# Nine buffers in place of three for the token rows of the input norm

## The chip, the cores and the metric

The kernel runs on one core of a Trainium2 chip. The metric is device time in microseconds (us) of one execution. Before the change three runs took 2201.86, 2203.27 and 2207.52 us, median 2203.27.

A core has five engines that each work through their own list of instructions in order: PE (TensorE, matrix multiplication), DVE (VectorE), ACT (ScalarE), POOL (GpSimd) and SP (SyncE, which here only issues transfers). They wait for each other by semaphores. Transfers between DRAM and the on-chip memory (SBUF) are moved by 16 DMA engines.

## The reference

One layer of a causal decoder over 16 meta tokens and 1024 real tokens of width 1024, all in float32:

```
h = concat(zeros(112), meta_tokens(16), x(1024))
u = rmsnorm(h, norm_mix_w)
z, xbc, dt, q, k, v, g_ssd, g_att = split(u @ w_in)          # 1024 x 8480
y_ssd = gated_rmsnorm(ssd(silu(conv4(xbc)), dt), z) @ w_ssd_branch
y_att = window_attention(q, k, v, rel_bias, sinks) @ w_attn_branch
h = h + (sigmoid(g_ssd+b0)*y_ssd + sigmoid(g_att+b1)*y_att) @ w_out
h = h + (silu(gate) * up) @ w_down      # (up, gate) = conv3(rmsnorm(h) @ w_ffn_in)
out = rmsnorm(h, norm_final_w)[:, 128:]
```

The attention looks at a window of 128 tokens, the meta tokens and a learned sink. The SSD branch (a state space model) goes through blocks of 128 tokens in order.

## The kernel before, in words

Matrices are split into a high and a low part (`split`, L94 to L96: ACT writes the high part, DVE subtracts and writes the low part), and each product is three matmuls: high by high (L168), low by high (L169) and high by low (L170). A projection job takes 128 columns of `w_in`: `prep` (L141) loads them into one of three `wf` buffers (512 KB, L145) and splits them into `wh` and `wl`; `gemm_slice` multiplies them with the normed tokens `r1h`, `r1l` in three slices of tokens, 24 matmuls each.

The head of the kernel is the loop that the change touches (L231 to L243). It goes over nine blocks of tokens: block 0 with the 16 meta tokens, blocks 1 to 8 with 128 rows of x (512 KB each). SP loads a block into `xt` (L234). `norm_T` then squares and sums it on ACT (L181), scales the sum on DVE (L182), takes its power on POOL (L183), multiplies the rows on DVE into `xn` (L184), transposes them in eight pieces on PE (L189, `ntp`), and splits them into `r1h` (ACT, L95) and `r1l` (DVE, L96). `xt` has three buffers, so a load has to wait until the block three before it has been normed. The loads of `norm_mix_w` (`wb`) and of the weights of K and V stand among those of x. The bias table of the attention (`rb`, `oh`, two matmuls `pg` at L223, `gv`) follows block 3, and the small constants (`rw`, `sel`, `d2`, `nsink`) follow the loop.

Behind the loop K and V are projected for all tokens (slices of 272, 384 and 384 tokens; the first needs blocks 0 to 2, the second 3 to 5, the third 6 to 8). K and V go to DRAM (`k_d`, `v_d`, stores of L294) and come back in another layout (`att_k` L498 in two halves of 1 MB, `att_v` L499, `att_vm` L501). Then 66 projection jobs follow, and between their matmuls run the attention (first matmuls `attS`, L574 and L575) and the SSD (per block: `ssdcb` L700, `ssdE` L708, `ssdpx` L717, `ssdyo` L751, `ssdst` L757, `ssdyd` L770, `ssdss` L789). After them come the branch products, the output projection, the gated MLP and the final norm.

The order of instructions is not written out by hand. A scheduler reads the whole program, plays it through with its own costs, and writes each engine's list; what is issued early or late in that play shifts where the background work (`pull`, attention and SSD) is set among the projections. It uses eight semaphores for transfers in turn: a transfer waits until the one issued eight places before it has landed.

```
            xt = p0.tile([P, D], F32, tag="xt", name="xt", bufs=3)
            sp.dma_start(xt[:n], A["meta_tokens"] if b == 0 else A["x"][P * (b - 1):P * b, :])
            if b in (2, 3):
                pend.append(prep(w_in[:, c0:c0 + P]))
            norm_T(xt, n, t0, wb, p0, ps0, "nt")
```

Of the kernel before, what the change touches and what calls it, by code (L numbers as in the profile page):

```python
# [11 lines left out]
F32 = mybir.dt.float32  # L12
# [6 lines left out]
P = 128  # L19
D = 1024  # L20
# [28 lines left out]
def blk(b):  # L49
    return (0, NM) if b == 0 else (NM + P * (b - 1), P)  # L50
# [36 lines left out]
def body(ctx: ExitStack, tc: tile.TileContext, A, out, keep=None):  # L87
# [52 lines left out]
    def prep(src, m=P, eng=None):  # L140
        wf = wp.tile([P, KC, P], F32, tag="wf", name="wf", bufs=3)  # L141
        wh = wp.tile([P, KC, P], F32R, tag="wh", name="wh", bufs=WB)
        wl = wp.tile([P, KC, P], F32R, tag="wl", name="wl", bufs=WB)
        q = abs(m)
        sp.dma_start(wf[:, :, :q], src.rearrange("(k p) c -> p k c", p=P))  # L145
        if m < 0:
            split(wh[:, :, :q], wh[:, :, q:2 * q], wf[:, :, :q])
        else:
            split(wh[:, :, :m], wl[:, :, :m], wf[:, :, :m], eng)
        return wh, wl, m  # L150
# [41 lines left out]
    def norm_T(xt, n, t0, wb, pl, psp, tagp):  # L192
        for ks, ps in norm_ps(xt, n, wb, pl, psp, tagp):
            split(r1h_[:, ks, t0:t0 + n], r1l_[:, ks, t0:t0 + n], ps)

    def rows(pl, psp, tagp, srcs, dst, name):
        n = sum(s.shape[0] for s in srcs)
        t = pl.tile([P, P], F32, tag="rows", name=name)
        o = 0
        for s in srcs:  # L200
            sp.dma_start(t[o:o + s.shape[0], :], s)
            o += s.shape[0]
        ps = psp.tile([P, 512], F32, tag=tagp, name="rowsT")
        pe.transpose(ps[:, :n], t[:n, :], ident[:n, :n])
        dve.tensor_copy(dst, ps[:, :n])
# [8 lines left out]
    def bias_by_distance(p0, ps0):  # L214
        rb = p0.tile([33, 16], F32, name="rb", bufs=1)
        oh = p0.tile([33, L_BAND + L_M1 + L_M31], F32, name="oh", bufs=1)
        dve.memset(rb, 1.0)
        sp.dma_start(rb[0:32, :], A["rel_bias"])
        sp.dma_start(oh, A["c_oh"])
        gv = p0.tile([16, L_BAND + L_M1 + L_M31], F32, name="gv", bufs=1)  # L220
        for o, n in ((0, 384), (384, 160)):
            pg = ps0.tile([P, 512], F32, tag="nt", name="pg")
            pe.matmul(pg[:16, :n], rb, oh[:, o:o + n], start=True, stop=True)  # L223
            dve.tensor_copy(gv[:, o:o + n], pg[:16, :n])
        sp.dma_start(gv_d, gv)
# [3 lines left out]
    with tc.tile_pool(name="p0", bufs=2) as p0, tc.tile_pool(name="ps0", bufs=4, space=PSUM) as ps0:  # L229
        wb = p0.tile([P, D], F32, name="wb", bufs=1)  # L230
        for b in range(9):  # L231
            t0, n = blk(b)
            xt = p0.tile([P, D], F32, tag="xt", name="xt", bufs=3)
            sp.dma_start(xt[:n], A["meta_tokens"] if b == 0 else A["x"][P * (b - 1):P * b, :])  # L234
            if b == 0:
                sp.dma_start(wb, A["norm_mix_w"].partition_broadcast(P))
            if b in (2, 3):
                c0 = C_K if b == 2 else C_V
                pend.append(prep(w_in[:, c0:c0 + P]))
            norm_T(xt, n, t0, wb, p0, ps0, "nt")  # L240
            if b == BD:
                bias_by_distance(p0, ps0)
        sp.dma_start(tri, A["c_tri"])  # L243
        cw = A["ssd_conv_w"].rearrange("t (c p) -> (t c) p", p=P)
        cb = A["ssd_conv_b"].rearrange("(c p) -> c p", p=P)
        rows(p0, ps0, "nt", [cw, cb], cvw, "rw1")
        dve.tensor_scalar(out=cvw, in0=cvw, scalar1=0.5, scalar2=None, op0=ALU.mult)
        rows(p0, ps0, "nt", [A["ssd_norm_w"].rearrange("(c p) -> c p", p=P),
                             A["gate_b"].rearrange("b (c p) -> (b c) p", p=P)], ngw, "rw2")
        dve.tensor_scalar(out=ngw[:, 16:32], in0=ngw[:, 16:32], scalar1=0.5, scalar2=None, op0=ALU.mult)  # L250
        fw = A["ffn_conv_w"].rearrange("t (c p) -> (t c) p", p=P)
        fb = A["ffn_conv_b"].rearrange("(c p) -> c p", p=P)
        rows(p0, ps0, "nt", [fw[0:88]], fcw[:, 0:88], "rw3")
        rows(p0, ps0, "nt", [fw[88:132], fb], fcw[:, 88:176], "rw4")
        sel = p0.tile([2, P], F32, name="sel", bufs=1)
        sp.dma_start(sel, A["c_sel"])
        d2 = p0.tile([2, 16], F32, name="d2", bufs=1)
        sp.dma_start(d2, A["ssd_d"].rearrange("(c e) -> e c", e=2))
        pd = ps0.tile([P, 512], F32, tag="nt", name="pd")
        pe.matmul(pd[:, :16], sel, d2, start=True, stop=True)  # L260
        dve.tensor_copy(dch, pd[:, :16])
        sp.dma_start(nsink, A["attn_sinks"].partition_broadcast(P))
        dve.tensor_scalar(out=nsink, in0=nsink, scalar1=-1.0, scalar2=None, op0=ALU.mult)
# [1059 lines left out]
```

## Time and profile before

| what | value |
|---|---|
| runs | 2201.86, 2203.27, 2207.52 us; median 2203.27 |
| profiled execution | 2204.14 us, of which the span of the trace is 2202.4 |
| PE | busy 2152.5 us, 98% of the span |
| DVE, ACT, POOL | busy 64%, 40%, 16% |
| granted TensorE clock, mean | 0.991 of full speed |
| DMA | 250.18 MB, 114 GB/s over the span |

Times in the rows are us from the start of the span. A line such as "[1.98 <-DMA nsink]" says how long an engine stood idle before an instruction and what it inferred as the last thing waited for. A PE that is busy is not always at its full clock: the column PEclk gives the share of full speed that was granted.

### The profile page before, as it was taken

What the parts mean: (1) busy time and instruction counts of PE and PEld (TensorE: products, weight loads), DVE (VectorE), ACT (ScalarE), POOL (GpSimd) and SP (SyncE); (2) the same over time, 40 slices, a digit from 0 to 9 for tenths busy, and PEclk for the clock granted to TensorE, in tenths of its full rate; (3) what the DMA queues carried; (4) which work ended last, traced back from release to release, by engine and by line L of the source; (5) the groups of instructions that cost most, each with busy time, mean ns of one, the idle gap of its engine ahead of it and who ended that gap; (6) DMA issues with size and microseconds to landing.
All of it is one profiled execution on the core that took longest, in us unless ns stands there. A gap on an engine that the chain in (4) does not pass through costs nothing. (4 is left out here: it accounts for less than half of the span.)

```text
span 2202.4 us, 35895 instructions
## 1 busy us (share of the span) xinstructions
PE 2152.5 (98%) x14090; PEld 2049.8 (93%) x14090; DVE 1405.1 (64%) x2558; ACT 871.5 (40%) x1701; POOL 361.3 (16%) x303
## 2 busy tenths in 40 slices
PE   7999999999999999999999999999999999989998
PEld 6899999999999999999999999878999999968887
DVE  6576665567775486354245644558888888875566
ACT  4455644446653454253322212324334333441112
POOL 1111111003330131022000000004433444200000
PEclk9999999999999999999999999999999999999999
DMA  6521422247663464364455432434222222353223
GB/s 172 135 74 47 122 73 72 81 110 182 148 149 95 115 160 114 97 155 115 162 164 165 144 96 84 135 115 125 87 76 78 78 86 68 106 182 96 86 67 125
DMA packets 300329, 250.18 MB, mean 114 GB/s; under 512 B 31768, under 2 KB 272306, under 8 KB 299391
## 3 DMA queue, kind: packets, MB, share of 16 engines
q1 hardware_dynamic: 300159, 247.88, 39.4%
q8 instruction: 111, 1.82, 0.3%
q14 instruction: 59, 0.48, 0.1%
HBM read 180.26 MB, written 67.57 MB: 113 GB/s over the span
## 5 line engine op out<-in xcount | busy, mean ns | idle before, releaser
L168 PE MATMUL gacc<-r1h,wh 128*128 128x342 f32 (+4 forms) x1776 | 579.9, 328 | 5.9 <-DVE cv L457 4.5
L169 PE MATMUL gacc<-r1l,wh 128*128 128x342 f32 (+4 forms) x1776 | 582.0, 328 | 2.1 <-DVE ss L182 1.7
L170 PE MATMUL gacc<-r1h,wl 128*128 128x342 f32 (+4 forms) x1776 | 579.0, 327 | 0.0
L168 PEld LDWEIGHTS gacc<-r1h,wh 128*128 128x128 f32 x1776 | 337.7, 190 | 10.2 <-issue 4.9
L169 PEld LDWEIGHTS gacc<-r1l,wh 128*128 128x128 f32 x1776 | 337.9, 190 | 5.8 <-DVE ss L182 1.9
L170 PEld LDWEIGHTS gacc<-r1h,wl 128*128 128x128 f32 x1776 | 338.0, 191 | 2.8 <-issue 0.2
L96 DVE TENSOR_TENSOR wl<-wf,wh 128x1024 fp32r<-128x1024 f32 x97 | 123.2, 1270 | 116.4 <-ACT wh L95 113.4
L95 ACT ACTIVATE wh<-wf 128x1024 fp32r<-128x1024 f32 x115 | 121.0, 1052 | 191.8 <-PE gacc L169 148.7
L457 DVE SCALAR_TENSOR_TENSOR cv<-gacc,cvw,cv 128x346 f32<-128x346 f32 (+2 forms) x216 | 123.8, 574 | 44.6 <-ACT cv L453 41.6
L1278 PE MATMUL dacc<-dh,r1l 128*128 128x512 f32 x336 | 132.3, 394 | 0.0
L1279 PE MATMUL dacc<-dl,r1h 128*128 128x512 f32 x336 | 132.2, 393 | 0.0
L1277 PE MATMUL dacc<-dh,r1h 128*128 128x512 f32 x336 | 131.9, 393 | 0.0
L1283 DVE TENSOR_TENSOR hh<-dacc,hh 128x512 f32<-128x512 f32 x128 | 87.4, 689 | 67.9 <-PE dacc L1279 66.9
L168 PE MATMUL gacc<-r2h,wh 128*128 128x342 f32 x384 | 122.7, 320 | 3.1 <-ACT r1h L95 1.5
L169 PE MATMUL gacc<-r2l,wh 128*128 128x342 f32 x384 | 123.1, 321 | 0.0
L170 PE MATMUL gacc<-r2h,wl 128*128 128x342 f32 x384 | 122.8, 320 | 0.0
L95 ACT ACTIVATE q<-q 128x1024 fp32r<-128x1024 f32 x44 | 46.7, 1061 | 143.9 <-PE uacc L1174 93.4
L183 POOL TENSOR_TENSOR ss<-ss,mhalf 128x1 f32<-128x1 f32 (+2 forms) x18 | 11.1, 617 | 480.7 <-DVE ss L182 470.3
L1144 POOL TENSOR_TENSOR q<-wf 128x512 f32<-128x512 f32 x22 | 67.7, 3076 | 121.0 <-DVE q L96 121.0
L770 PE MATMUL ssdyd<-M,ssdxd 128*128 128x128 f32 (+1 forms) x576 | 79.9, 272 | 0.0
L770 PEld LDWEIGHTS ssdyd<-M,ssdxd 128*128 128x128 f32 (+1 forms) x576 | 76.3, 191 | 2.5 <-issue 0.8
L1189 DVE SCALAR_TENSOR_TENSOR ta<-ra,fcw,ta 128x1024 f32<-128x1024 f32 x44 | 78.0, 1772 | 0.0
(436 smaller groups left out, 5283.2 us busy)
## 6 DMA issues: line engine op xcount, KB each, us to landing
wf<-in_w_in SPq DMA_DIRECT2D x66, 512.0 KB
wf<-in_w_ffn_in SPq DMA_DIRECT2D x44, 512.0 KB
gl<-ga_d SPq DMA_DIRECT2D x72, 171.0 KB
a_d<-ta SPq DMA_DIRECT2D x22, 512.0 KB
wf<-a_d SPq DMA_DIRECT2D x22, 512.0 KB
wf<-in_w_ffn_out SPq DMA_DIRECT2D x22, 512.0 KB
xs_d<-xt SPq DMA_DIRECT2D x16, 520.0 KB
z_d<-zt SPq DMA_DIRECT2D x16, 513.0 KB
```

The lines of the kernel that those rows point to most:

```text
L95: act.activation(hi, src, AF.Copy)
L96: (eng or dve).tensor_tensor(out=lo, in0=src, in1=ff(hi), op=ALU.subtract)
L168: pe.matmul(ps[:m, :n], wh[:, k, :m], rh[k][:, t0:t0 + n], start=k == 0, stop=False)
L169: pe.matmul(ps[:m, :n], wh[:, k, :m], rl[k][:, t0:t0 + n], start=False, stop=False)
L170: pe.matmul(ps[:m, :n], wl[:, k, :m], rh[k][:, t0:t0 + n], start=False, stop=k == KC - 1)
L457: dve.scalar_tensor_tensor(out=t[:, z:m], in0=ps[:, off + z - lag:off + m - lag], scalar=w, in1=t[:, z:m], op0=ALU.mult, op1=ALU.add)
L770: pe.matmul(yd[:, j, :n], u.xd[:n, j, 64 * e:64 * e + P], u.M[:n, i * n:(i + 1) * n], start=e == 0, stop=e == 1)
L1189: dve.scalar_tensor_tensor(out=t, in0=row[:, 2 - lag:2 - lag + SEQ], scalar=w, in1=t, op0=ALU.mult, op1=ALU.add)
L1277: pe.matmul(ps, ah[:, tb], wh[:, cs], start=i == 0, stop=False)
L1278: pe.matmul(ps, al[:, tb], wh[:, cs], start=False, stop=False)
L1279: pe.matmul(ps, ah[:, tb], wl[:, cs], start=False, stop=i == len(cur) - 1)
L1283: dve.tensor_tensor(out=hh[:, b, cs], in0=ps, in1=hh[:, b, cs], op=ALU.add)
```

## The change

The tile `xt` gets nine buffers in place of three, 36 KB per partition in place of 12 KB, so no load of x waits for a norm to release a buffer.

```diff
--- before.py
+++ after.py
@@ -230,7 +230,7 @@
         wb = p0.tile([P, D], F32, name="wb", bufs=1)
         for b in range(9):
             t0, n = blk(b)
-            xt = p0.tile([P, D], F32, tag="xt", name="xt", bufs=3)
+            xt = p0.tile([P, D], F32, tag="xt", name="xt", bufs=9)
             sp.dma_start(xt[:n], A["meta_tokens"] if b == 0 else A["x"][P * (b - 1):P * b, :])
             if b == 0:
                 sp.dma_start(wb, A["norm_mix_w"].partition_broadcast(P))
```

The scheduler writes other lists from it. The instructions are the same in number and kind on every engine. Their order differs in the first part of the program, up to about the seventeenth `ssdss` of 36, and from there on it is the same on all five engines. Four places:

On SP at the start of the program, the loads in the order of issue (`-` before, `+` now):

```order
 L234 DMA xt<-in_x 128x1024 x2
-L145 DMA wf<-in_w_in 128x8x128 x2
+L145 DMA wf<-in_w_in 128x8x128
+L234 DMA xt<-in_x 128x1024
+L145 DMA wf<-in_w_in 128x8x128
 L218 DMA rb<-in_rel_bias 32x16
 L219 DMA oh<-c_oh 33x544
+L234 DMA xt<-in_x 128x1024 x5
 L243 DMA tri<-c_tri 128x128
 L201 DMA rw_331<-in_ssd_conv_w 96x128
-L234 DMA xt<-in_x 128x1024
```

The third block of x is now asked for ahead of V's weights (the second `wf`), and the last five blocks ahead of all the small constants. Since a transfer waits for the one eight places before it, `nsink`, eight places behind the last block of x, waits for that block to land.

On DVE in the changed kernel, from the low part of block 3 to the low part of block 4 (`gv` is the bias table, `ss` and `xn` in the middle are block 5's):

```order
L96 TENSOR_TENSOR r1l<-ntp,r1h 128x4x128
L224 COPY gv<-pg 16x384
L263 TENSOR_SCALAR nsink<-nsink 128x16
L182 TENSOR_SCALAR ss<-ss 128x1
L184 SCALAR_TENSOR_TENSOR xn<-xt,ss,wb 128x1024
L224 COPY gv<-pg 16x160
L96 TENSOR_TENSOR r1l<-ntp,r1h 128x4x128 x2
```

The small operation on `nsink`, which needs its transfer, now stands ahead of the norm of block 5. Before it stood at this place ahead of the one of block 3:

```order
L96 TENSOR_TENSOR r1l<-ntp,r1h 128x4x128 x2
L182 TENSOR_SCALAR ss<-ss 128x1
L263 TENSOR_SCALAR nsink<-nsink 128x16
L96 TENSOR_TENSOR r1l<-ntp,r1h 128x4x128
L182 TENSOR_SCALAR ss<-ss 128x1
L184 SCALAR_TENSOR_TENSOR xn<-xt,ss,wb 128x1024 x2
```

On SP around the reloading of K and V, before:

```order
L544 DMA tab<-gv_d 128x2x256
L546 DMA tab<-gv_d 128x2x16
L145 DMA wf<-in_w_in 128x8x128
L294 DMA v_d<-vs 128x512
L294 DMA v_d<-vs 128x128
L498 DMA att_k<-k_d 64x2x2048 x2
L501 DMA att_vm<-v_d 16x64 x2
L508 DMA att_t_399<-gv_d 8x16
```

and now:

```order
L294 DMA v_d<-vs 128x512
L501 DMA att_vm<-v_d 16x64 x2
L294 DMA v_d<-vs 128x128
L542 DMA tab<-gv_d 128x2x16
L498 DMA att_k<-k_d 64x2x2048 x2
L543 DMA tab<-gv_d 128x2x128
L499 DMA att_v<-v_d 128x8x64
L544 DMA tab<-gv_d 128x2x256
L546 DMA tab<-gv_d 128x2x16
L145 DMA wf<-in_w_in 128x8x128
```

The reload of K now stands ahead of the tables and of the weights of a later job, and that of V follows two places behind it. On PE the first `attS` stands behind 246 projection matmuls, before behind 267.

On PE in the SSD of the second of four groups, before (`ssdyd` of one block of 128 tokens, then parts of the next two):

```order
L770 MATMUL ssdyd<-M,ssdxd_5152 128x128 x8
L708 MATMUL ssdE<-ssdR_5155,ssdL_5156 128x512
L717 MATMUL ssdpx<-ident,xs 128x128 x4
L789 MATMUL ssdss<-ones,qs 128x1
L751 MATMUL ssdyo<-bc,ssdh 128x128 x4
L708 MATMUL ssdE<-ssdR_5160,ssdL_5161 128x512
L700 MATMUL ssdcb<-bc 128x128
L703 MATMUL ssdcb<-ident,bc 128x128
L168 MATMUL gacc<-r1h,wh 128x342
L169 MATMUL gacc<-r1l,wh 128x342
```

and now, behind the same `ssdyd`:

```order
L708 MATMUL ssdE<-ssdR_5160,ssdL_5161 128x512
L789 MATMUL ssdss<-ones,qs 128x1
L757 MATMUL ssdst<-xe_7665,bt_7642 128x512
L757 MATMUL ssdst<-xe_7664,bt_7643 128x512
L717 MATMUL ssdpx<-ident,xs 128x128 x4
L708 MATMUL ssdE<-ssdR_5160,ssdL_5161 128x512
L708 MATMUL ssdE<-ssdR_5155,ssdL_5156 128x512
L751 MATMUL ssdyo<-bc,ssdh 128x128 x4
L700 MATMUL ssdcb<-bc 128x128
L703 MATMUL ssdcb<-ident,bc 128x128
L770 MATMUL ssdyd<-M,ssdxd_5151 128x128 x8
L168 MATMUL gacc<-r1h,wh 128x342
```

Before, 24 projection matmuls stood between that `ssdyd` and the next one; now none does, and 264 of them follow in one piece.

## Rows read from the trace of the kernel before

**Rows 1.** Busy time by stretch: us of each engine, (instructions), PEclk, DMA share, GB/s

```profile
0.00:50.00 50.00, 36.43 (x217) 33.10 (x218) 30.18 (x59) 24.21 (x44) 6.68 (x17) 0.97 0.63 171
50.00:100.00 50.00, 44.87 (x277) 44.35 (x276) 22.70 (x65) 21.44 (x55) 4.98 (x3) 0.93 0.62 146
100.00:636.00 536.00, 535.39 (x3568) 515.92 (x3566) 362.54 (x964) 289.33 (x738) 89.88 (x95) 1.00 0.40 103
636.00:650.00 14.00, 13.46 (x98) 12.57 (x97) 12.65 (x24) 10.85 (x26) 5.66 (x6) 1.00 0.54 128
...
718.00:2202.40 1484.40, 1454.37 (x9494) 1376.53 (x9493) 937.62 (x1383) 501.87 (x799) 249.73 (x176) 0.99 0.38 114
```

**Rows 2.** Waits of PE, whole run: us in total, times, longest

```profile
PE ntp L189 <- DVE xn L184: 8.3, 3, 7.7
PE attS L574 <- DMA att_v<-v_d: 5.1, 1, 5.1
PE gacc L168 <- DVE cv L457: 4.5, 2, 4.1
...
PE gacc L169 <- DVE ss L182: 1.7, 1, 1.7
```

**Rows 3.** Timeline of the head: start, duration, engine, line, operation, [idle before <-releaser]

```profile
1.19 0.42 SPq L234 DMA_DIRECT2D xt<-in_meta_tokens  x1
...
3.34 1.05 ACT L181 ACTIVATE xn<-xt 16x1024 f32<-16x1024 f32 x1 [1.32 <-DMA xt<-in_meta_tokens]
...
12.70 1.06 ACT L95 ACTIVATE wh<-wf 128x1024 fp32r<-128x1024 f32 x1
...
14.15 0.43 SPq L262 DMA_DIRECT2D nsink<-in_attn_sinks  x1
...
17.07 0.40 PE L169 MATMUL gacc<-r1l,wh 128*128 128x272 f32 x1 [1.67 <-DVE ss L182]
...
19.06 0.17 DVE L263 TENSOR_SCALAR nsink<-nsink 128x16 f32<-128x16 f32 x1 [1.98 <-DMA nsink<-in_attn_sinks]
...
29.89 0.62 PE L168 MATMUL gacc<-r1h,wh 128*128 128x384 f32 x2 [1.39 <-ACT r1h L95]
```

**Rows 4.** Groups of instructions, 0 to 50 us: count, busy us, mean ns

```profile
L184 DVE SCALAR_TENSOR_TENSOR xn<-xt,ss,wb 128x1024 f32<-128x1024 f32 (+1 forms) x9 | 11.5, 1281 | 4.8 <-POOL ss L183 3.0 <-DMA wb<-in_norm_mix_w 1.7
...
L96 DVE TENSOR_TENSOR wl<-wf,wh 128x1024 fp32r<-128x1024 f32 x2 | 2.4, 1216 | 0.0
```

**Rows 5.** Busy time by stretch, two us of the head

```profile
10.00:12.00 2.00, 1.08 (x5) 1.09 (x6) 1.26 (x3) 1.18 (x3) 0.56 (x1) 1.00 1.17 289
```

**Rows 6.** Timeline around the first attention matmul

```profile
59.25 0.47 SPq L145 DMA_DIRECT2D wf<-in_w_in  x1
...
61.44 1.94 SPq L498 DMA_DIRECT2D att_k<-k_d  x2
...
77.20 0.46 PE L574 MATMUL attS<-att_k,qx 128*128 128x144 f32 x1 [5.13 <-DMA att_v<-v_d]
```

**Rows 7.** Waits of SP's queue, 50 to 100 us

```profile
SPq L145 <- DMA att_k<-k_d: 5.1, 1, 5.1
```

**Rows 8.** Busy time by stretch, behind that wait

```profile
78.00:83.00 5.00, 5.00 (x19) 5.00 (x19) 3.15 (x12) 2.89 (x10) 0.19 (x1) 0.50 0.83 211
```

**Rows 9.** Groups of instructions of DVE by shape, 636 to 656 us

```profile
L714 DVE TENSOR_TENSOR M<-M,cbm 128x1024 f32<-128x1024 f32 x2 | 2.4, 1214 | 0.0
L96 DVE TENSOR_TENSOR xe<-xe,xe 128x512 fp32r<-128x512 f32 x3 | 2.2, 728 | 1.9 <-ACT xe L95 1.9
L772 DVE TENSOR_TENSOR y<-ssdyd,y 128x512 f32<-128x512 f32 x3 | 2.0, 681 | 0.0
...
L96 DVE TENSOR_TENSOR bt<-ssdcb,bt 128x128 fp32r<-128x128 f32 x2 | 0.6, 280 | 0.0
```

**Rows 10.** Timeline of PE in the SSD: one `ssdyo` and the next

```profile
637.45 1.05 PE L751 MATMUL ssdyo<-bc,ssdh 128*128 128x128 f32 x8
...
641.63 1.14 PE L751 MATMUL ssdyo<-bc,ssdh 128*128 128x128 f32 x8
```

## The prediction

> **What bounds the kernel now.** I read the busy time by stretch first [rows 1]. PE is busy for all but 13.6 us of the first 50, 5.1 us of the next 50, 0.6 us from 100 to 636 and 0.5 us from 636 to 650; from 718 on it idles 30.0 us of 1484. So the kernel is one long row of matmuls, and a change to loads can win at most what PE loses to waiting, and to a low clock, in the part that it moves. The orders of the two kernels are the same on every engine behind the seventeenth ssdss, which stands near 718 us in this trace; I take the 30.0 us behind it as unchanged. What can move is 19.8 us of idle time ahead of it, nearly all of it in the first 100 us.
>
> The list of PE's waits [rows 2] says which waits these are. 7.7 us is the start, up to the first normed rows: meta tokens, norm_mix_w, first transposes. Nothing of that moves, since those loads keep their places. 5.1 us is the first matmul of the attention. The small ones lie between 10 and 30 us: 1.7 us at 17.07 and 1.4 us at 29.89 [rows 3]. From 30 us to the end of K and V PE is full.
>
> So loads of x do not bound the head as a whole: they cost PE some 3 us. What the change buys there is small, and the question is what the new order does elsewhere.
>
> **The change part by part.** First the head. The third block of x now goes ahead of V's weights. Around there the DMA engines are full and move 289 GB/s [rows 5], so 512 KB (0.524 MB) ahead costs V's weights 1.8 us. Their split began at 12.70 at the latest [rows 3] and now begins near 14.5. In the new order DVE does V's low part (1.22 us) and then the norm of block 3 (1.28 us, [rows 4]) ahead of the low part of block 2, which PE's third matmul needs; with the split on ACT (1.06 us, [rows 3]) that is 14.5 + 1.06 + 1.22 + 1.28 = 18.1. Then PE goes on, first with transposes and a bias matmul that stood further back and are no loss. Before, PE went on at 17.07. Cost: 1.0 us.
>
> In the trace a small transfer waits for what is ahead of it: nsink, 8 KB, was issued at 14.15 and used at 19.06, 4.9 us later, while the meta tokens, 64 KB with little ahead of them, took 2.15 us from issue to use [rows 3]. The Trainium skill says the same (DMA: Bandwidth & Descriptors, section "Queues, rings and completion order"): on each DMA engine descriptors are taken in the order of the ring. It speaks against this change, since a load asked for early delays one that is needed sooner; the trace agrees with its 4.9 us. Without the rule the first term would be 0 instead of 1.0.
>
> Next, nsink. It waits for the last block of x to land. Up to there some 5.97 MB have to be moved (wb, eight blocks, two weights of 0.524 MB each, and about 0.2 MB of small ones); at 289 GB/s from 2 us on that is near 22.6. With 2.15 us for itself nsink lands near 24.8. DVE reaches its operation near 23 (an estimate from the durations of what stands ahead), so DVE waits some 2 us in front of the norm of block 5; before it waited 1.98 us [rows 3]. PE needs block 5 for the second slice of K, and has 21 matmuls of the first slice left and block 6's transposes to put in between. Against this the wait of 1.4 us at 29.89 goes, since blocks 4 to 8 are there early; what is late next is DVE, which has the norms and low parts of four blocks to do. I take -0.4 for the two together, so +0.6 for the head. Bounds: -3.1 (both waits of 1.7 and 1.4 gone and no other in their place) and +3.8 (nsink as slow as before, 2.75 us more, with the 1.0).
>
> Second, the reload of K. The wait of 5.1 us is put down to att_v, but attS reads att_k, and the transfer that SP itself was held by until the same moment is att_k [rows 7]: its second half. It was issued at 61.44, and attS began at 77.20 [rows 6], 15.8 us for 2 MB behind the weights of a later job (issued at 59.25) and half of V. In the new order these weights and three tables come behind it. 2.1 MB of K, 0.52 of weights and 0.33 of V in 15.8 us are 187 GB/s, at which the weights alone are 2.8 us. att_k is issued when the stores of K have landed, which I put near 59.3, so 2.1 us earlier. 77.2 - 2.8 - 2.1 = 72.3. PE came to attS at 77.20 - 5.13 = 72.07; it now comes 21 matmuls earlier, at 0.150 us each (535.39 us for 3568, [rows 1]) 3.2 us, and loses some 0.5 us on the transposes of V, which stand two matmuls behind the projection that they read. So it comes at 69.4 and waits 2.9 us in place of 5.1: -2.2, and +0.5 for V's transposes, -1.7 in all. Bounds: the wait goes and with it the stretch at half clock behind it: from 78 to 83 us the granted clock was 0.50 (1.2 GHz of 2.4) and 19 matmuls took 5.0 us in place of 2.9 [rows 8], so -5.1 - 2.1 = -7.2. Above: att_k lands no earlier, PE waits 77.2 - 69.4 = 7.8, +2.7, with the 0.5 it is +3.2. I take -1.7: a wait of 3 us still follows on an idle PE, and the low clock stays.
>
> Third, the SSD of group 2, near 636 to 650 us. This is the tightest place of the long middle: DVE is busy 12.65 of 14 us, and PE idles 0.5 [rows 1]. One block costs DVE 1.21 + 0.73 + 6 of 0.68 + 2 of 0.28 = 6.6 us [rows 9], PE 4.18 from one ssdyo to the next [rows 10], and with ssdcb and a second ssdE, which lie outside, about 4.8. As long as projection matmuls stand between, PE has work while DVE catches up. In the new order the 24 between two ssdyd have moved behind: two blocks go through with no projection between. Their surplus is 2 x (6.6 - 4.8) = 3.6 us; the score tile M has two buffers, so DVE works one block ahead, and I take half, +1.8. Bounds: 0 (DVE far enough ahead) and +4.1, the longest wait for DVE in the jobs [rows 2].
>
> The rest of the reshuffled order from 100 to 718 us shows nothing as tight: the smallest distances between an attention score and its transposes, counted in columns of projection, are no smaller than before. I take 0, with 1 us either way. In the reserved memory there is no cost: the attention's tiles that lie over the larger pool are first used past 43 us, when all of x has been normed.
>
> Sum: 0.6 - 1.7 + 1.8 = +0.7 on the profiled execution's 2204.14, which is 2204.8. That execution lies 0.87 above the median of the runs shown, so I predict 2204.0.
>
> **The rivals.** (a) The first attention wait goes for good: att_k lands by the time PE comes, and the clock stays up. For it: three transfers less ahead, 5.1 us of wait and 2.1 us of low clock to win. Against it: PE comes 2.7 us earlier too, and the DMA engines are full over the whole stretch. -7.2 + 0.6 + 1.8 = -4.8: 2198.5; with no loss in the SSD 2196.7.
>
> (b) The early loads are hidden and the head gains its waits: -3.1 in place of 0.6, the rest as forecast, -3.0: 2200.3. For it: two waits on blocks of x are in the trace. Against it: DVE and ACT are in order, and the new place of nsink. The Trainium skill's rule for authors (DMA: Bandwidth & Descriptors, section "Rules for kernel authors"), to issue a DMA early and wait late, would give this time. The trace bears it out only in part: PE had work at most of these times.
>
> (c) Slower: the uncovered SSD blocks. If DVE is a full block behind when PE comes there, each ssdyd waits for the mask product and for the scaled x of its own block, PE loses 4.1 us, and an idle PE can come back at half clock, as behind 77 us, for another 2.1 us. It decides from the point at which DVE's backlog exceeds one block. With 0.6 and no gain at att_k: +6.8, 2210.1.
>
> (d) Nothing changes: the loads are capped at eight in flight, since each waits for the one eight places before, so "all in one go" is five at once at most behind the weights. That is within the forecast's band.
>
> **How the numbers follow.** Forecast 0.60, (a) 0.12, (b) 0.12, (c) 0.16. The measurement of this kernel can tell about 0.3%, 6.6 us, from no change: below 2196.7 is faster, above 2209.9 slower. Forecast and (b) lie inside nearly always, (a) reaches the lower bound in less than half of its cases, (c) the upper in most. Faster 0.09, same 0.76, slower 0.15. The range goes from (a) without a loss in the SSD, 2197, to a little beyond (c), 2212.
>
> **What would show it.** In the changed profile: the split of V's weights begins past 14 us; DVE waits for nsink near 23 to 25 us; K's last matmul ends within 2 us of where it did; attS waits 2 to 4 us, near 69 to 73, with PEclk at 0.50 behind it; PE idles 2 to 3 us in the stretch with the back-to-back ssdyd; behind the seventeenth ssdss the same 30 us of idle time. I am wrong if attS waits under 1 us (then a), or if one of the middle stretches idles over 4 us (then c).

## The result, and the profile of the changed kernel

The changed kernel takes 2221.96 us in the median of six runs (2217.67 to 2223.57), the kernel before 2202.71 in as many (2199.50 to 2207.52). The ratio is 1.0078, 95% interval 1.0068 to 1.0088: about 19 us slower, where 2204.0 was forecast with a range of 2197 to 2212. The profiled execution of the changed kernel took 2218.29 us, its span is 2216.5 us, 14.1 more than before.

I read the busy time by stretch first, as before [rows 1]. Changed kernel: stretch, its length, busy us and instructions of PE, PEld, DVE, ACT, POOL, then the granted clock, DMA share, GB/s.

```profile
0.00:50.00 50.00, 37.41 (x217) 33.60 (x218) 29.33 (x56) 24.23 (x44) 6.64 (x17) 1.00 0.59 171
50.00:100.00 50.00, 45.31 (x282) 44.33 (x280) 26.46 (x78) 23.09 (x62) 5.15 (x4) 0.93 0.60 146
...
225.00:255.00 30.00, 22.46 (x136) 21.21 (x135) 16.27 (x59) 15.26 (x47) 3.68 (x6) 0.89 0.62 142
...
640.00:680.00 40.00, 35.74 (x226) 34.15 (x225) 29.72 (x48) 22.52 (x46) 9.86 (x12) 0.91 0.56 135
...
0.00:1056.40 1056.40, 1022.47 (x6701) 990.45 (x6701) 651.41 (x1470) 511.26 (x1202) 175.44 (x198) 0.98 0.44 114
1056.40:2216.50 1160.10, 1136.51 (x7392) 1065.27 (x7390) 759.08 (x1089) 356.84 (x499) 184.44 (x105) 0.99 0.35 112
```

The same of the kernel before, for the stretches that stand out:

```profile
225.00:255.00 30.00, 29.39 (x194) 28.19 (x193) 20.62 (x65) 20.15 (x59) 5.53 (x6) 1.00 0.73 177
640.00:680.00 40.00, 39.45 (x259) 38.65 (x259) 26.47 (x47) 18.19 (x37) 8.64 (x10) 1.00 0.46 130
...
0.00:1039.90 1039.90, 1016.00 (x6699) 985.38 (x6700) 647.57 (x1470) 514.53 (x1202) 174.17 (x198) 0.99 0.45 116
1039.90:2202.40 1162.50, 1136.53 (x7393) 1064.37 (x7390) 757.55 (x1089) 357.00 (x500) 187.18 (x105) 0.99 0.35 112
```

The last two rows of each are cut at the last ssdrs, the end of the SSD: 1039.9 us before, 1056.4 after, 16.5 later with the same 6700 matmuls ahead. Of that, PE idles 10.0 us more (33.9 against 23.9) and is busy 6.5 us longer. Behind the cut the changed kernel is 2.4 us shorter. The first 100 us are not where it goes: PE idles 1.4 us less there (82.72 us busy, 81.30 before). Little of that is progress: the first score of the attention starts at 73.78 in place of 77.20, 3.4 us earlier, but behind 21 matmuls fewer, which are 3.2 us [rows 1]. So some 0.3 us were won up to there (an estimate from these rows). The loss sits in two stretches that the prediction had passed over or priced low: 225 to 255 us (PE 6.9 us less busy, granted clock 0.89 against 1.00) and 640 to 680 us (3.7 less, 0.91 against 1.00).

The waits of PE in the changed kernel, whole run (total, times, longest), beside [rows 2]:

```profile
PE ntp L189 <- DVE xn L184: 9.8, 4, 8.0
...
PE attS L574 <- DMA att_k<-k_d: 5.3, 1, 5.3
...
PE attS L574 <- issue: 4.3, 1, 4.3
...
PE ssdE L708 <- DMA ssdL<-cs_d: 3.3, 1, 3.3
PE attS L636 <- ACT p0t L634: 2.3, 1, 2.3
```

The 4.3 is the first score of the attention, 5.1 before. Three are new: a second wait for att_k of 5.3 (before it was 0.61), one of 2.3 for p0t, one of 3.3 for ssdL. Their places in PE's timeline of the changed kernel (start, duration, what, idle before it and what ended it):

```profile
230.56 0.17 PE L618 MATMUL attS<-att_k,att_q 128*16 128x16 f32 x1
...
235.09 0.18 PE L632 MATMUL attS<-ident,p__2749 16*16 16x16 f32 x1
237.55 0.28 PE L636 MATMUL attS<-p0t,att_vm 16*64 16x16 f32 x2 [2.28 <-ACT p0t L634]
...
245.86 0.46 PE L574 MATMUL attS<-att_k,qx 128*128 128x144 f32 x1 [5.26 <-DMA att_k<-k_d]
...
653.15 0.49 PE L708 MATMUL ssdE<-ssdR,ssdL 128*128 128x512 f32 x1
656.97 0.77 PE L708 MATMUL ssdE<-ssdR,ssdL 128*128 128x512 f32 x1 [3.33 <-DMA ssdL<-cs_d]
```

**The first place** is the second load of K. One tile att_k serves both groups of heads. L618, the meta tokens' score, is the last reader of the first group's K; only behind it may the second group's be loaded (L498), and L574 is the first reader. In the order of the changed kernel 16 projection matmuls stand between the two, in the order of before 55. Both kernels need about the same time from the issue of the load to the score. Before:

```profile
234.02 0.17 PE L618 MATMUL attS<-att_k,att_q 128*16 128x16 f32 x1
...
234.22 1.24 SPq L498 DMA_DIRECT2D att_k<-k_d  x2
...
248.34 0.31 PE L574 MATMUL attS<-att_k,qx 128*128 128x144 f32 x1 [0.61 <-DMA att_k<-k_d]
```

After, L498 is issued at 231.14, so 14.7 us to the score against 14.1: the load takes about as long, and PE has 39 projection matmuls less to do meanwhile. The transpose of the meta rows (L632) and the product that needs its copy (L636), with 19 projection matmuls between them before, now stand side by side, and PE waits out ACT's copy of the transpose, `p0t`.

**The second place** is the end of the SSD's group 1, the second of its four. Each block has two ssdE. Between the ssdE of four successive blocks the changed order has 3, 0 and 0 projection matmuls; before, the same gaps held 69, 0 and 312. Behind each place the clock is at its lower level, 1.2 GHz of 2.4. Changed kernel, same columns as the first fence:

```profile
74.00:79.00 5.00, 5.00 (x19) 5.00 (x20) 2.02 (x9) 1.11 (x5) 0.19 (x1) 0.50 1.01 237
...
245.80:249.70 3.90, 3.84 (x15) 3.69 (x16) 2.16 (x7) 0.49 (x1) 0.00 (x0) 0.50 0.58 169
656.90:663.00 6.10, 6.03 (x29) 5.97 (x29) 4.60 (x8) 2.44 (x6) 2.05 (x3) 0.52 0.42 100
```

The first row answers to [rows 8]; the other two are new, and at half clock they cost (1 - 0.50) x 3.9 = 2.0 and (1 - 0.52) x 6.1 = 2.9 us. With 6.9 and 3.7 us of idle time that is 8.9 for the first place and 6.6 for the second, 15.5 us. With the 0.3 won ahead of them, 1.3 of the 16.5 are left. Of these 0.8 are idle time between 255 and 600 us (PE is busy 344.19 of 345 us there, 345.00 before), and some 0.5 are without a place.

### The profile page after: what moved, and what is told of

It reads as the page before. It is cut to its first block, busy times and chain, and to the rows that moved or that the text cites. A ratio compares the mean times of both kernels' runs of the same rounds, so it can differ in the third digit from the quotient of the medians.

```text
span 2216.5 us, 35918 instructions
## 1 busy us (share of the span) xinstructions
PE 2159.0 (97%) x14090; PEld 2055.7 (93%) x14090; DVE 1410.5 (64%) x2558; ACT 868.1 (39%) x1701; POOL 359.9 (16%) x303
## 5 line engine op out<-in xcount | busy, mean ns | idle before, releaser
L726 POOL TENSOR_TENSOR xe<-ssdxd,dec 128x512 f32<-128x512 f32 (+1 forms) x32 | 36.8, 1149 | 310.3 <-DVE ssdxd L721 309.9
```

## The experiments

Theory O: the early loads cost nothing; the loss comes from the order that the scheduler made of them, at these two places. Theory L: the early loads themselves, or the larger pool, cost the time. The leads (AHEAD_BG, set in pull) move the attention's work, its loads with it, against the projections and change no instruction, so they give either kernel nearly the other's order. "Reload" below is the count of projection matmuls between the two readers of att_k, "SSD" the three gaps between blocks at the end of group 1; each kernel was compared with the kernel before on the same chip in five rounds (medians of the kernel before there: 2204.37 for e1 to e4, 2203.04 for e5 to e8, 2205.23 for e9 to e12).

| run | buffers, edit | reload | SSD | us | ratio to before (95%) |
|---|---|---|---|---|---|
| before | 3 | 55 | 69, 0, 312 | 2202.71 | |
| after | 9 | 16 | 3, 0, 0 | 2221.96 | 1.0078 (1.0068 to 1.0088) |
| e1 | 5 | 55 | 69, 0, 312 | 2204.33 | 0.9997 (0.9988 to 1.0006) |
| e2 | 6 | 16 | 3, 0, 0 | 2221.21 | 1.0072 (1.0059 to 1.0084) |
| e3 | 3, lead 200 | 17 | 3, 0, 0 | 2223.11 | 1.0082 (1.0069 to 1.0094) |
| e4 | 9, lead 175 | 48 | 69, 0, 312 | 2206.89 | 1.0013 (1.0004 to 1.0022) |
| e5 | 3, lead 165 | 55 | 3, 0, 0 | 2214.41 | 1.0052 (1.0038 to 1.0066) |
| e6 | 9, one block's lead 100 | 16 | 70, 0, 312 | 2211.98 | 1.0040 (1.0028 to 1.0053) |
| e7 | 3, first block's lead 120 | 55 | 69, 0, 312 | 2201.87 | 0.9997 (0.9988 to 1.0005) |
| e8 | 9, first block's lead 120 | 55 | 69, 0, 312 | 2200.74 | 0.9991 (0.9982 to 1.0001) |
| e9 | e5 with a third ssdR, ssdL | 55 | 11, 0, 0 | 2207.31 | 1.0013 (1.0003 to 1.0023) |
| e10 | e8, att_k in two pieces | 55 | 69, 0, 312 | 2200.84 | 0.9981 (0.9973 to 0.9990) |
| e11 | e7, att_k in two pieces | 55 | 69, 0, 312 | 2201.24 | 0.9981 (0.9972 to 0.9990) |
| e12 | 9, att_k in two pieces | 48 | 69, 0, 312 | 2196.47 | 0.9960 (0.9947 to 0.9974) |

### Loads or order: e1 to e4

```
e1, e2   -  xt = p0.tile([P, D], F32, tag="xt", name="xt", bufs=3)
         +  xt = p0.tile([P, D], F32, tag="xt", name="xt", bufs=5)     (e2: 6)
e3       -  AHEAD_BG = 170
         +  AHEAD_BG = 200                                             (bufs=3)
e4       +  bufs=9 and AHEAD_BG = 175
```

> Five buffers for xt in place of three. Theory O (the order): the time lost with nine buffers, 14 us between the two profiled executions, sits where the new order has less projection work: 230 to 250 us (reload of K for the second group of heads: 16 projection matmuls between the last reader of the old K and the first of the new, 55 before) and 650 to 663 us (three SSD blocks with 3, 0 and 0 projection matmuls between their ssdE). With five buffers the order differs from that of three only in the head; at these places it is as before, 55 matmuls and one gap of 0. O expects 2201 to 2206. Theory L (the early loads themselves, or the larger pool, cost the time): two of the six extra buffers, so about a third of 19 us, 2209.

> Six buffers for xt. Its order of matmuls is that of nine buffers, row for row (16 matmuls at the reload of K; 3, 0, 0 in the SSD). Theory O: the whole loss is there at once, 2218 to 2224, a step between five and six buffers. Theory L: half of the loss, 2212.

> Three buffers as before, so no early loads and no larger pool; AHEAD_BG, the lead that the attention gets in the order, is 200 in place of 170. This order has 17 projection matmuls at the reload of K and 3, 0, 0 in the SSD, like that of nine buffers. Theory O: the same two stalls, PE idle 6 to 8 us near 230 to 250 and 3 to 5 us near 650, time 2215 to 2224. Theory L: 2200 to 2206.

> Nine buffers, and AHEAD_BG 175 in place of 170. This order has 48 projection matmuls at the reload of K, 12 between the two transposes of the meta rows (none with nine buffers alone), and the SSD as before. Theory O: both stalls gone, 2200 to 2207. Theory L: the loads are as early as in the changed kernel, 2218 to 2224.

All four times came out as theory O had it. Between five and six buffers the time steps by 17 us at once, and six are as slow as nine. Three buffers with the bare order are as slow as nine, with the same three waits. The one for K is shorter (3.4 us in place of 5.3; PE idles 5.7 us from 225 to 255, a little under the 6 to 8 expected), the granted clock there lower (0.83 in place of 0.89). PE's waits of e3, 100 to 720 us:

```profile
PE attS L574 <- DMA att_k<-k_d: 3.4, 1, 3.4
PE ssdE L708 <- DMA ssdL<-cs_d: 3.2, 1, 3.2
PE attS L636 <- ACT p0t L634: 2.3, 1, 2.3
```

Nine buffers with both places covered are 0.13% above the kernel before; e4's reload, with 48 matmuls, still waits 1.8 us for att_k.

### What each place costs: e5 and e6

```
e5       -  AHEAD_BG = 170
         +  AHEAD_BG = 165                                             (bufs=3)
e6 (bufs=9; at.step counts the calls in pull, 36 is the first block of the fifth pair)
         -  with tc.high_priority(AHEAD_SSD if sd.on else AHEAD_BG):
         +  lead = AHEAD_SSD if sd.on else FIRST.get(at.step, AHEAD_BG)
         +  with tc.high_priority(lead):
         ...
         +  FIRST = {0: 170, 36: 100}
```

> Three buffers, AHEAD_BG 165. The reload of K for the second group keeps its 55 projection matmuls; the SSD has the bare blocks of nine buffers (3, 0, 0 projection matmuls between their ssdE). It prices the SSD place alone. Theory O, from the trace of nine buffers: PE idles 3.7 us more there, and the 16 ssdyd, 8 ssdyo and others behind it run at half clock, some 2.9 us: 6.6 us, so 2209 to 2213. Rival: the reload of K made the whole difference, 2202 to 2206.

> Nine buffers; the first block of the second group's first pair gets a lead of 100 in place of 170, nothing else. This order has 16 projection matmuls at the reload of K and none between the two transposes of the meta rows, as with nine buffers alone; the SSD has no three bare blocks (19, 17, 70, 0, 312). It prices the reload alone. Theory O: 6.9 us more idle and some 1.7 us of half clock at 230 to 250, less 1.4 us won in the first 100 us: 2209 to 2214. Rival (the SSD made the difference): 2201 to 2205.

Each place stalls alone where it alone is bare. PE's waits of e5, 600 to 720 us:

```profile
PE ssdE L708 <- DMA ssdL<-cs_d: 3.4, 1, 3.4
...
```

PE's waits of e6, 100 to 720 us (its lines from L142 on stand 1 to 4 further down):

```profile
PE attS L578 <- DMA att_k<-k_d: 5.4, 1, 5.4
PE attS L640 <- ACT p0t L638: 2.3, 1, 2.3
```

The SSD alone costs 11.4 us by the medians (interval 8 to 15), above the 6 to 10 that I expected; the reload with nine buffers costs 8.9 (6 to 12), as expected. Together 20.3, against 19.3 for the changed kernel: within these intervals the two places account for the whole of it. In e5's profile, 8.2 us longer than before, the place shows 3.7 us of idle time and, from 651 to 656, a granted clock of 0.66, 1.7 us, so some 5.4; from 505 to 515 the clock is 0.76 and 0.90 with PE busy throughout, another 1.7. For that see the last section.

### Which link in the SSD: e9

```
(AHEAD_BG = 165, bufs=3)
-  for i in range(2):                     R = s.tile(..., name=f"ssdR{i}"), L = s.tile(..., name=f"ssdL{i}")
+  for i in range(3):
...
-  R = sd.R[b % 2] if b else sd.R0        L = sd.L[b % 2]
+  R = sd.R[b % 3] if b else sd.R0        L = sd.L[b % 3]
```

> As the run that had the SSD place alone bare (three buffers, AHEAD_BG 165), with three sets of ssdR and ssdL in place of two, so that the rows of cs_d for a block can be loaded while two blocks are in work. The three SSD blocks are still bare (11, 0, 0 projection matmuls between their ssdE; 55 at the reload of K). Theory D (the link is the reload of ssdL: it waits for the last ssdE of the block two before, then for SP and the DMA queue): the wait of 3.4 us on cs_d goes and most of the half clock behind it, 2204 to 2209. Theory V (DVE's backlog, as the prediction had it): a wait of 3 to 4 us on M or ssdxd comes in its place, 2211 to 2215.

Theory D stands. All that PE waits for in e9 from 600 to 720 us:

```profile
PE ssdst L757 <- DMA g_d<-gt__7712: 1.0, 1, 1.0
PE ssdyd L770 <- DVE M L714: 0.3, 1, 0.3
```

The wait on cs_d is gone, DVE's work has not taken its place, and e9 stands 0.13% above the kernel before where e5 stood 0.52%: some 9 of its 11 us came back, although the blocks stand nearly as bare as there (11 matmuls ahead of them in place of 3, some 1.3 us). So the link is the reload of this pair of tiles. e9 gives a third buffer to both; that ssdL is the one that binds is read from PE's wait in e5. SP's queue in the changed kernel shows why it is late:

```profile
650.25 0.37 SPq L145 DMA_DIRECT2D wf<-in_w_in  x1
650.92 0.42 SPq L694 DMA_DIRECT2D ssdR<-cs_d  x1
651.43 1.24 SPq L748 DMA_DIRECT2D ec<-ecs_d  x2
652.73 0.83 SPq L696 DMA_DIRECT2D ssdL<-cs_d  x2
```

A set of ssdR and ssdL is free when the ssdE of the block two before has run; ssdR for it is asked for at once. The few KB of ssdL are issued 1.8 us later, behind two pieces of ec, stand in line behind these and a weight tile of 512 KB, and PE goes on at 656.97, 4.2 us after their issue. The Trainium skill (DMA: Bandwidth & Descriptors, section "Queues, rings and completion order") has the DMA engines take descriptors in the order of their ring; these 4.2 us agree with it, as nsink's 4.9 did [rows 3].

### Early loads in a covered order, and a shorter first load: e7, e8, e10 to e12

```
e7, e8   FIRST = {0: 120} as in e6, with 3 and 9 buffers
e10-e12  -  for half in (slice(0, 64), slice(64, 128)):
         -      sp.dma_start(ff(at.k[half]), k_d[:, r].rearrange("i p t -> p i t"))
         +  for cs in (slice(1904, 2048), slice(0, 1904)):
         +      for half in (slice(0, 64), slice(64, 128)):
         +          sp.dma_start(ff(at.k[half])[:, :, cs], k_d[:, r, cs].rearrange("i p t -> p i t"))
```

> Three buffers; the very first block of the attention gets a lead of 120 in place of 170, which puts 18 more matmuls (2.7 us) ahead of its first score; the reload of K and the SSD are as before (55; 1, 22, 69, 0, 312). Theory: the wait for the first K falls from 5.1 to about 2.4 us and the half clock behind it may stay: 2200 to 2202, 2199 if the clock stays up. Rival: the loads of K get the lower lead too and land later, so nothing is won: 2203 to 2206.

> The same lead of 120 for the first block, with nine buffers. Both places are covered as in the kernel before (55; 1, 22, 69, 0, 312), and the loads of x are all early. Theory O: early loads are worth what the first 100 us showed, 1.4 us; 2198 to 2203, at or below three buffers with the same lead. Rival (early loads cost time by themselves, as 2206.89 for nine buffers with both places covered may hint): 3 us above three buffers with the same lead.

> Nine buffers with the first block's lead of 120, and att_k loaded in two pieces: the 144 columns of the first block first, the other 1904 behind. Both places are covered (55; 1, 22, 69, 0, 312). If the wait for K is the time of the whole megabyte, the first score no longer waits and the rest has some 30 matmuls more to land: PE idles 2 us or less near 75, 2195 to 2200. Rival: the wait only moves to the second block's score, 2199 to 2203.

> The same split of att_k and lead of 120 with three buffers. Against the run with nine it prices the early loads of x when nothing behind them is bare: by the first 100 us of the changed kernel nine are 1.4 us better, so 2197 to 2202 here. Rival (early loads hold up the small ones): three are as fast or faster.

> Nine buffers, leads as in the changed kernel (170), only att_k in two pieces. The shorter first load alone gives an order with 48 projection matmuls at the reload of K, 12 between the transposes of the meta rows, and the SSD as before (1, 22, 69, 0, 312); the first score stands 46 rows earlier than with the lead of 120. Theory O: neither place stalls over 2 us although all loads of x are early, 2197 to 2205. Rival (the early loads cost the time): 2215 or more.

Where the orders of the middle are alike, nine buffers and three differ by 1.1 us (e8 and e7) and 0.4 us (e10 and e11), less than the intervals can tell. The rule that the prediction weighed, to issue a load early and wait late (the Trainium skill, DMA: Bandwidth & Descriptors, section "Rules for kernel authors"), brings nothing here that these runs can see: PE had other work at most times when blocks of x came late. e7's gain is not measurable either. e10 missed its range, by 0.8 us: the wait for K went, and 3.3 us for DVE's qy came 4 us behind the first score. Its trace shows what holds qy up. ACT waits 9.7 us for att_vm, a small load that SP issues at 62.85, right behind two pieces of att_k (61.56), and the copies that qx and qy need stand behind it on ACT:

```profile
77.09 0.31 ACT L507 ACTIVATE att_v<-att_vm 32x128 fp32r<-32x128 f32 x1 [9.72 <-DMA att_vm<-v_d]
```

In e12 att_vm is issued at 58.84, ahead of these pieces, and ACT waits 2.2 us for it. e12 keeps the lead of 170 and splits the load. It is 0.4% faster than the kernel before, some 9 us, and 0.5 us below the range expected. Part of that is again the order, which covers both places (48; 69, 0, 312). e4, with nine buffers, a lead of 175, the same counts and K loaded whole, stands 0.13% above the kernel before, so against e4 the split is worth some 11 us. Rows of e12, columns as in the first fence:

```profile
50.00:100.00 50.00, 47.68 (x309) 45.96 (x308) 29.66 (x88) 26.04 (x67) 6.38 (x5) 1.00 0.62 149
225.00:255.00 30.00, 30.00 (x199) 28.61 (x198) 23.25 (x76) 18.29 (x57) 3.13 (x5) 1.00 0.60 144
```

Of the 5.1 us at the first score [rows 6] 1.9 are left, by its list of waits at the second block; the clock stays up behind them, and PE does not idle at the reload. The split does more than shorten the first load; it gives each piece its own last reader. SP's issues of att_k in e12:

```profile
43.84 1.35 SPq L499 DMA_DIRECT2D att_k<-k_d  x2
...
61.32 1.24 SPq L499 DMA_DIRECT2D att_k<-k_d  x2
...
222.11 1.24 SPq L499 DMA_DIRECT2D att_k<-k_d  x2
...
233.51 1.98 SPq L499 DMA_DIRECT2D att_k<-k_d  x2
```

The transfers at 43.84 and 233.51 are the small pieces (72 KB each), those at 61.32 and 222.11 the large ones (952 KB each). The first small pieces come 17 us ahead of the large ones. At the reload the large ones go first, behind the last score of the old group (a matmul that starts at 221.79), and only the small ones wait for the meta score at 227.17; the first reader starts at 240.04 without a wait. Whether three buffers with the split load and the lead of 170 would do as well was not run.

## Why the prediction was wrong

**The head: right in what happens, at a cost of 0.1 us in place of 0.6.** DVE waits for nsink at 23.92, in the 23 to 25 forecast, and PE goes on at 18.34 where 18.1 was worked out. PE's timeline of the changed kernel, and DVE's, beside [rows 3]:

```profile
18.34 1.94 PE L189 MATMUL ntp<-ident,xn 128*128 128x128 f32 x8 [1.24 <-DVE xn L184]
...
23.92 0.18 DVE L263 TENSOR_SCALAR nsink<-nsink 128x16 f32<-128x16 f32 x1 [0.88 <-DMA nsink<-in_attn_sinks]
```

But DVE's wait is 0.88 in place of 2, and the wait of 1.4 us at 29.89 is gone with nothing in its place. PE is busy 37.41 of the first 50 us, before 36.43. Yet it gets no further: the transposes of V (pvt), the first work behind the matmuls of K and V, start at 51.60 before and at 51.73 now.

```profile
51.60 0.82 PE L412 MATMUL pvt<-ident,vt 128*16 128x128 f32 x6
```

```profile
22.45 0.43 PE L169 MATMUL gacc<-r1l,wh 128*128 128x272 f32 x1
...
30.06 0.29 PE L169 MATMUL gacc<-r1l,wh 128*128 128x272 f32 x1
...
51.73 0.82 PE L412 MATMUL pvt<-ident,vt 128*16 128x128 f32 x6
```

The idle time saved went into slower matmuls: in the changed kernel one of 272 columns takes 0.43 us at 22.45 and 0.29 at 30.06, though the granted clock of 0 to 50 us is given as 1.00. Before, the slow ones end at 21.67, now at 24.26. Busy time by itself is not progress.

**The first load of K: right in what happens, mis-sized: -0.4 us in place of -1.7.** PE came to the first score at 69.5 (forecast 69.4), waited 4.3 us (forecast 2.9, with 2 to 4 as the sign), and the half clock stayed behind it. att_k was issued at 60.88, 0.6 us earlier than before and not 2.1. The wait is 0.9 us shorter, and V's transposes wait 0.4 (0.5 forecast). Head and K together won some 0.3 us up to the first score; the sum had 1.1.

```profile
60.88 1.35 SPq L498 DMA_DIRECT2D att_k<-k_d  x2
...
73.78 0.46 PE L574 MATMUL attS<-att_k,qx 128*128 128x144 f32 x1 [4.26 <-issue]
```

**The SSD: the place right, the link and the size wrong.** +1.8 was taken, with bounds 0 and +4.1; by the trace it is 3.7 us of idle time and 2.9 of half clock, and alone it measured 11.4 (8 to 15). Three blocks are bare, not two. Rival (c) had its size, 4.1 and 2.1, but it too put the wait on DVE. The step that failed is "the score tile M has two buffers, so DVE works one block ahead": it looked at one pair of buffers of the block, and the pair that binds is ssdR and ssdL, whose way back goes through SP and a DMA.

**The rest of the order: this is what put the time out of the range.** The step reads "shows nothing as tight: the smallest distances between an attention score and its transposes, counted in columns of projection, are no smaller than before. I take 0, with 1 us either way". It counted one kind of distance, from a producer to its consumer within a block. The distance that shrank is the other kind, from the last reader of a single buffer to the first reader of its next content, with 14 us of load between them. The prediction had the length of that load in its own second step, 15.8 us from issue to score [rows 6], and 55 matmuls at 0.150 us are 8.3 us of cover, 16 are 2.4. That alone would have given about 6 us of idle time; e6 prices the place at 8.9.

**Behind the SSD: right.** The last ssdrs to the end takes 1160.1 us against 1162.5; the 2.4 less are idle time.

The direction had 0.15 for slower, carried by rival (c). No rival had the reload. The last sign, over 4 us of idle time in one of the middle stretches, came true (7.5 us from 225 to 255, 4.3 from 640 to 680), but it pointed at (c) alone, and the larger of the two is not (c)'s place.

## What to carry to other kernels

Where a scheduler makes the order, a change of a buffer count is a change of the order, and its price is set wherever a long load into a single buffer lost its cover, hundreds of us from the edit. So list the single and double buffers that a DMA refills, and count for each the work between the last reader of the old content and the first of the new, in the new order, against the load's time in the trace. Such a place can be mended at the load, with a third buffer or with pieces that have readers of their own: e9 stands some 9 us below e5 and e12 some 11 below e4, each with nearly the same counts of cover.

## What was not expected of the hardware

A stall cost 2 to 3 us more through the clock: 5.3 us of idle time were followed by 3.9 us at half clock, 3.3 by 6.1. The length of the idle time alone does not decide it. The wait of 1.8 us in e4 was followed by half clock too:

```profile
249.00:251.00 2.00, 2.00 (x11) 1.86 (x9) 0.27 (x1) 0.78 (x3) 0.00 (x0) 0.50 0.86 265
```

The 1.9 us of e12 and the 1.0 of e9 were followed by none, nor was the wait of 2.3 us for p0t in the changed kernel. The same wait in e3, 2.3 us too, was: from 239 to 243 its clock stands at 0.56 and 0.58. And the clock also falls where PE had no idle time at all. In e6, with PE busy 345.00 of 345 us from 255 to 600:

```profile
510.00:515.00 5.00, 5.00 (x25) 4.83 (x26) 2.77 (x6) 3.38 (x9) 1.40 (x3) 0.66 0.60 178
515.00:520.00 5.00, 5.00 (x35) 4.63 (x34) 2.79 (x6) 3.09 (x9) 0.00 (x0) 1.00 0.82 169
```

25 matmuls in 5 us in place of 35. What PE did before it is block 0 of an SSD group, the one with the 16 meta tokens, whose matmuls are small:

```profile
508.00 1.95 PE L774 MATMUL ssdyd<-M,ssdxd 16*128 16x16 f32 x16
```

This holds throughout. In stretches of 1 us from 26 to 1100 us the fourteen profiles have 34 falls with no idle time in the 7 us before, and each begins within 1.5 us of the end of such small ssdyd matmuls: behind block 0 of the fourth group in all fourteen, of the third in twelve, of the first in six, of the second in two. The kernel before has two of them. No run changes these blocks, so that they set it off is likely and not shown, and why some blocks do and others do not is open. e5's stretch from 505 to 515 is one; whether such stretches make the rest of e5's excess and the 6 us between runs of one kernel, no run here shows.
